# A transformer layer with product-key experts: 672 dense and 352 gathered tokens instead of 704 and 320, five sums kept in PSUM instead of two, gates in DRAM by four blocks

## The chip, the core and the metric

The kernel runs on one core of a Trainium2 chip. The metric is device time in microseconds (us) of the whole program. The engines are TensorE (PE, its weight loads PEld), VectorE (DVE), ScalarE (ACT), GpSimd (POOL) and SyncE (SP), which issues most of the DMAs.

## The reference

One decoder layer on 1024 tokens of width 1024, all in float32. First a modulation from a conditioning vector, a norm, a mixing of tokens (four heads of a gated recurrence, four groups of a short convolution) and its projection. Then the expert layer, which takes most of the time: each token chooses 8 x 16 of 16384 experts by product keys, and each expert is one row of U and one of V:

```python
q = (xb @ w_query).reshape(T, PEER_HEADS, 2, PEER_HALF)
s = jnp.einsum('thpk,hpnk->thpn', q, sub_keys)          # scores of 2 x 128 keys
top_s, top_i = lax.top_k(s, PEER_TOPK)                  # 16 of each half
cand_s = top_s[:, :, 0, :, None] + top_s[:, :, 1, None, :]
best_s, best_pos = lax.top_k(cand_s.reshape(T, PEER_HEADS, -1), PEER_TOPK)
gate = jax.nn.softmax(best_s, axis=-1)
act = jax.nn.gelu(jnp.einsum('td,thkd->thk', xb, u), approximate=False)
return jnp.einsum('thk,thkd->td', gate * act, v)
```

A residual, a second modulation and a final norm close the layer.

## The kernel before

Every large product runs as three products of float32r halves (high x high, high x low, low x high), so one step over 128 channels is three matmuls.

The tokens are treated in two ways. The **dense** ones (the last TD = 704) meet all 128 blocks of 128 experts: a gate matrix that is zero for experts that a token has not chosen is multiplied onto the activations. The **gathered** ones (the first REST = 320) fetch their chosen rows of U and V from DRAM by indirect DMA, 128 rows of 4 KB at a time, one expert for each of up to 128 tokens. A group of 128 tokens needs 128 fetches of U and 128 of V. The last group has only 64 tokens; they are laid twice over the partitions (`dup`), each copy takes half of their experts, and 64 + 64 fetches do; a small matmul (`fold`) adds the copies.

The dense tokens lie in two column parts, `SPL`: 384 columns and the rest. The work goes like this:

- **Mixing** of both halves of the sequence, norms, and the queries of gathered tokens (`query`, on `hg2`).
- **Dense queries and top-k** (lines 873 and 922 to 926).
- **Gates**: 64 tokens at a time (`TG`), one-hot products on TensorE give each token's gates over all 16384 experts; `stg` collects them and one DMA puts them into DRAM (`gd`), in the order in which the main loop reads them back, `GB` blocks of experts at a time. Meanwhile `u_early` computes the activations of 40 blocks (every third) ahead, which wait in DRAM (`ged`).
- **The main loop** over 128 blocks of experts. `u_steps` (line 1161) computes a block's activations for all dense tokens: 24 matmuls into a PSUM bank `pa` for each column part, then Gelu on ScalarE; early blocks come from `ged` instead. `w_step` multiplies by the gates (line 1376, from the buffer `gsb`) and splits the result into `Wh` and `Wl` (lines 113, 114). `v_load` fetches and splits the block's rows of V. After every three blocks (`SB`) comes a **V phase**, `v_phase`: 16 groups (2 column parts x 8 blocks of output channels), each of 9 matmuls (line 1395) into a PSUM bank; VectorE then adds the bank to a sum `acc` in SBUF (line 1411). The sums listed in `FIXED` stay in PSUM banks of their own (`pacc`) for the whole loop and need no addition.
- **The background**, strewn over the main loop by `advance` and `along`: for each gathered row GpSimd issues the fetch into one of five buffers (line 1082, four `grow_` and `more`), and VectorE takes a dot product with the token (line 1100, a u row) or adds the weighted row to a sum (line 1092, a v row).

A scheduler in the recording layer orders the instructions of each engine ahead of time; engines then run their queues in order.

PSUM has eight banks. In the main loop they are two for `pa`, one for each fixed sum, and the others rotate as `pv`:

```python
FIXED = [(0, 0), (1, 0)]
PV = 6 - len(FIXED)
def new_pv():
    return psM.tile([P, 512], F32, name="pv", bufs=PV)
```

Of the kernel before, what the change touches and what calls it, by code (L numbers as in the profile page):

```python
# [7 lines left out]
F32 = mybir.dt.float32  # L8
# [11 lines left out]
P = 128  # L20
# [12 lines left out]
TD = 704  # L33
# [4 lines left out]
GG = [(t, min(P, REST - t)) for t in range(0, REST, P)]  # L38
NG = len(GG)
# the gathered tokens of the last, half tile get their experts together with the half tile of the others  # L40
FULL = REST // P
LAST = REST % P
assert LAST and LAST == P - TD % P
SB = 3
GB = 2
# [9 lines left out]
NF = 2.1  # L55
# [7 lines left out]
FIXED = [(0, 0), (1, 0)]  # L63
# [34 lines left out]
def build(tc, A, out, dbg=None):  # L98
# [12 lines left out]
    def split(hi, lo, src):  # L111
        """two parts of 12 bits each"""
        C.activation(hi, src, AF.Copy)  # L113
        V.tensor_tensor(lo, src, hi.bitcast(F32), op=OP.subtract)  # L114

    def raw_tile(pl, shape, name, lb):
        """float32 values that wait for their split, in a buffer of the low parts"""
        return pl.tile(shape, F32R, name=name + "l", bufs=lb).bitcast(F32)
# [7 lines left out]
    def rsqrt(r, v, tmp, e=0):  # L126
        """of v / 4 ** e: a first guess from the exponent, then Newton steps"""
# [12 lines left out]
    with root:  # L140
# [23 lines left out]
        # ---------------------------------------------------------------- the background  # L164
        # top-k of the gathered tokens, then their experts row by row: steps of it are strewn over the other work;
        # a step yields what it costs VectorE
# [10 lines left out]
        # ---------------------------------------------------------------- stationary operands  # L177
        # all of [P, KC, P], in the order in which TensorE takes them; each is fetched two and split one ahead
# [24 lines left out]
        def halve(n):  # L203
            """there is a third set of halves at times"""
# [7 lines left out]
        def deepen(pl, first, n, every):  # L212
            """that many more from the first on: one of so many goes into a pool of its own"""
# [18 lines left out]
        def ahead():  # L232
            """in the midst of the products with one: split the next"""
# [5 lines left out]
        # ---------------------------------------------------------------- constants, modulation  # L239
# [4 lines left out]
        # three buffers of four row tiles, in turn of the normalised input or w_out, and of the mix or the residual  # L244
# [36 lines left out]
        # TensorE gets to its full clock while the first loads are under way  # L281
# [29 lines left out]
        def mod_part(sec, wa, d):  # L311
            """some columns of a section of the modulation"""
# [5 lines left out]
        def mod_part_rows(sec, wa, d):  # L318
            """the same on TensorE, as a row that is turned into columns"""
# [28 lines left out]
        # ---------------------------------------------------------------- norm 1 and the values  # L348
# [14 lines left out]
        def lnT1(xs, pl, k, h1, onact=False):  # L363
            """transpose a column block of the four row tiles, scale, shift and split it"""
# [16 lines left out]
        def wi_load(pl, k, lb=3, hb=2, ahead=0, wait=[]):  # L381
            """loads run ahead of the splits"""
# [34 lines left out]
        # ---------------------------------------------------------------- projections, token mixing  # L417
# [6 lines left out]
        # lower bounds  # L424
# [16 lines left out]
        # a window of 32 columns of it holds ones in one of them  # L441
# [12 lines left out]
        def mixing(half, mods, h1, og):  # L454
            """projections, recurrence, convolution and group norms of half a sequence, into og"""
# [43 lines left out]
            # blocks of w_in: per head f, q, g (0..11), per conv group c, x, b (12..23)  # L499
# [54 lines left out]
            # masks of the levels: the highest bit in which s and t differ, for s < t  # L554
# [117 lines left out]
            def finish(g):  # L672
                """the scales of a group, from the rows of all of them"""
# [18 lines left out]
        # ---------------------------------------------------------------- w_out, norm 2  # L692
# [4 lines left out]
        def w_out(yp, wop, half, og, finish, between=None, after=None):  # L697
            """the residual after the token mixing, normalised row tiles"""
# [834 lines left out]
```

## Time and profile before

| | us |
|---|---|
| median of 3 runs | 2983.33 (2979.0 to 2987.94) |
| profiled execution, span | 2982.4 (no other time of it is given) |
| TensorE, busy | 2902.0 |
| VectorE, busy | 2524.2 |
| ScalarE, busy | 946.0 |
| GpSimd, busy | 796.2 |
| DRAM read and written | 706.5 MB |

A matmul counts as busy from its start to its modelled end, and neighbours overlap; how fast they follow each other is read from their starts. A VectorE instruction, too, is listed longer than the distance at which the next can start. Busy shares are means over stages with different limits, so the sections below go by stage.

### The profile page before, as it was taken

The page shows a single profiled execution, that of the slowest core. Times are in us where ns is not written, and L with a number is a line of the kernel's source. Part 1 is how long each engine was busy: PE and PEld are TensorE (multiplying, and loading weights), DVE is VectorE, ACT ScalarE, POOL GpSimd, SP SyncE. Part 2 cuts the span into 40 slices and gives each one's busy share as a digit, 9 for nine tenths or more (in the row PEclk, how much of TensorE's full clock was granted, in tenths as well). Part 3 has the DMA queues.
Part 4 walks back from the last instruction along what each step waited for, and adds up shares of the span by engine and source line. Part 5 has one row for each costly group of instructions (what it writes and reads, how often), then busy time and mean ns, then how long its engine had stood idle before and what let it go on. Part 6 is the DMA issues. An engine that isn't in the chain of part 4 may idle for free.

```text
span 2982.4 us, 47131 instructions
## 1 busy us (share of the span) xinstructions
PE 2902.0 (97%) x18242; PEld 2750.8 (92%) x18242; DVE 2524.2 (85%) x5314; ACT 946.0 (32%) x1541; POOL 796.2 (27%) x661
## 2 busy tenths in 40 slices
PE   8999999999999999999999999999999999999998
PEld 6887888878999899999999999999999999999997
DVE  6885559988999877568889989889989988989987
ACT  5643655433122444422222222222222221222221
POOL 0000000000000000015454445435545444444450
PEclk8999999989999999999999999999999999999999
DMA  7424342244223577778889888889889888889883
GB/s 269 146 88 142 130 142 71 85 146 147 61 89 108 181 238 241 234 257 299 302 305 335 314 309 327 320 304 336 304 306 325 319 317 318 307 318 332 304 311 128
DMA packets 286898, 709.65 MB, mean 238 GB/s; under 512 B 26513, under 2 KB 124817, under 8 KB 284370
## 3 DMA queue, kind: packets, MB, share of 16 engines
q1 hardware_dynamic: 192994, 365.56, 35.5%
q0 software_dynamic: 93680, 341.09, 32.2%
q8 instruction: 142, 2.33, 0.3%
q14 instruction: 82, 0.67, 0.1%
HBM read 633.65 MB, written 72.88 MB: 237 GB/s over the span
## 4 chain that ended last, share of the span: by engine, by line
PE 64%; DVE 17%; DMA 10%; issue 5%; ACT 2%; POOL 1%; SPq 0%; DVEq 0%; ACTq 0%; POOLq 0%
PE pv L1395 22%; PE pa L1161 19%; PE pp L467 6%; DMA wl<-in_uT 5%; PE pq L873 4%; PE pacc L1395 3%; DVE wl L114 2%; DMA Wl<-ged 2%; PE ps L577 1%; PE pp L873 1%; PE pg L1327 1%; PE pp L378 1%; DVE gacc L1092 1%; PE pp L714 1%; DVE acc L1411 1%
## 5 line engine op out<-in xcount | busy, mean ns | idle before, releaser
L1161 PE MATMUL pa<-h2h,wh 128*128 128x384 f32 (+1 forms) x1840 | 598.4, 325 | 2.7 <-ACT ge L1166 2.6
L1161 PE MATMUL pa<-h2h,wl 128*128 128x384 f32 (+1 forms) x1840 | 593.9, 323 | 0.0
L1161 PE MATMUL pa<-h2l,wh 128*128 128x384 f32 (+1 forms) x1840 | 593.7, 323 | 0.0
L1395 PE MATMUL pv<-Wh,vh 128*128 128x384 f32 (+1 forms) x1792 | 580.6, 324 | 11.7 <-DVE acc L1411 11.1
L1395 PE MATMUL pv<-Wl,vh 128*128 128x384 f32 (+1 forms) x1792 | 577.3, 322 | 0.0
L1395 PE MATMUL pv<-Wh,vl 128*128 128x384 f32 (+1 forms) x1792 | 577.0, 322 | 0.0
L1395 PEld LDWEIGHTS pv<-Wh,vh 128*128 128x128 f32 x1792 | 336.9, 188 | 22.4 <-DVE acc L1411 19.6
L1161 PEld LDWEIGHTS pa<-h2h,wh 128*128 128x128 f32 x1840 | 346.0, 188 | 4.5 <-ACT ge L1166 3.8
L1161 PEld LDWEIGHTS pa<-h2l,wh 128*128 128x128 f32 x1840 | 346.2, 188 | 0.0
L1161 PEld LDWEIGHTS pa<-h2h,wl 128*128 128x128 f32 x1840 | 346.0, 188 | 0.3 <-DVE wl L114 0.3
L113 ACT ACTIVATE Wh<-Wl 128x704 fp32r<-128x704 f32 x128 | 101.6, 793 | 747.8 <-PE pv L1395 588.2
L1395 PEld LDWEIGHTS pv<-Wh,vl 128*128 128x128 f32 x1792 | 337.0, 188 | 0.0
L1395 PEld LDWEIGHTS pv<-Wl,vh 128*128 128x128 f32 x1792 | 336.9, 188 | 0.0
L113 ACT ACTIVATE wh<-wl 128x1024 fp32r<-128x1024 f32 x187 | 198.0, 1059 | 420.8 <-DMA wl<-in_uT 205.2
L114 DVE TENSOR_TENSOR wl<-wl,wh 128x1024 fp32r<-128x1024 f32 x187 | 227.8, 1218 | 97.7 <-ACT wh L113 95.9
L1411 DVE TENSOR_TENSOR acc<-acc,pv 128x320 f32<-128x320 f32 (+1 forms) x574 | 286.1, 513 | 11.6 <-PE pv L1395 11.3
L114 DVE TENSOR_TENSOR vl<-vl,vh 128x1024 fp32r<-128x1024 f32 x128 | 156.0, 1219 | 18.3 <-ACT vh L113 18.2
L113 ACT ACTIVATE vh<-vl 128x1024 fp32r<-128x1024 f32 x128 | 134.6, 1052 | 79.5 <-DMA vl<-in_v 45.4
L467 PE MATMUL pp<-h1h,wh 128*128 128x512 f32 x384 | 156.6, 408 | 0.0
L467 PE MATMUL pp<-h1h,wl 128*128 128x512 f32 x384 | 152.5, 397 | 3.5 <-DVE wl L114 3.4
L1376 DVE TENSOR_TENSOR Wl<-Wl,gsb 128x704 f32<-128x704 f32 x128 | 113.2, 885 | 48.4 <-DMA Wl<-ged 36.9
L467 PE MATMUL pp<-h1l,wh 128*128 128x512 f32 x384 | 152.3, 397 | 0.0
(1778 smaller groups left out, 5978.2 us busy)
## 6 DMA issues: line engine op xcount, KB each, us to landing
wl<-in_uT SPq DMA_DIRECT2D x128, 512.0 KB
vl<-in_v SPq DMA_DIRECT2D x128, 512.0 KB
gd<-stg SPq DMA_DIRECT2D x11, 4096.0 KB
gsb<-gd SPq DMA_DIRECT2D x64, 704.0 KB
wl<-in_win SPq DMA_DIRECT2D x48, 512.0 KB
wa<-in_wada SPq DMA_DIRECT2D x16, 1024.0 KB
wl<-in_wq SPq DMA_DIRECT2D x32, 512.0 KB
ged<-ge SPq DMA_DIRECT2D x40, 352.0 KB
```

The source lines that it names most:

```text
L113: C.activation(hi, src, AF.Copy)
L114: V.tensor_tensor(lo, src, hi.bitcast(F32), op=OP.subtract)
L378: T.matmul(pvs[t], l[:, t * P:(t + 1) * P], r, start=(k == 0 and l is h1[0][k] and r is wi[0]), stop=(k == KC - 1 and l is h1[1][k]))
L467: T.matmul(pp, l[:, k], r[k], start=(i == 0), stop=(i == 3 * KC - 1))
L577: T.matmul(ps_[:, c], X[:, cs_], Y[:, cs_], start=True, stop=True)
L714: T.matmul(pm, l[:, t * P:(t + 1) * P], r, start=(k == 0 and l is yh[k] and r is woh[k]), stop=(k == KC - 1 and l is yl[k]))
L873: T.matmul(pq[:, :m], l[:, k], hs[k, r][:, o:o + m], start=(i == 0), stop=(i == 3 * KC - 1))
L1092: V.scalar_tensor_tensor(ac, r, aw[:, j:j + 1], ac, op0=OP.mult, op1=OP.add))
L1161: T.matmul(pa[:, :n], l[:, k], h2[k, r][:, o:o + n], start=(i == 0), stop=(i == 3 * KC - 1))
L1376: V.tensor_tensor(gv, gv, gs[b // GB][:, :, b % GB], op=OP.mult)
L1395: T.matmul(pv[:, :n], l[:, c * P:(c + 1) * P], r[:, o:o + n], start=(i == 0 and (not fx or b0 == 0)), stop=(i == 3 * (b1 - b0) - 1 and (no ...
L1411: V.tensor_tensor(a, a, pv[:, :n], op=OP.add)
```

## The change

TD goes from 704 to 672, so the dense parts are 384 and 288 columns, and 352 tokens are gathered. Of these, 96 don't fill a group of 128; they are split into 64 (twice over the partitions) and 32 (four times). There are 352 instead of 320 steps of the background, each one fetch of U and one of V, and a fourth group's end. Gates are built 32 tokens at a time, since 672 is no multiple of 64 tokens; `GB = 4` keeps the runs that they write into DRAM at the same length, and the main loop reads them for four blocks at once. Five sums instead of two stay in PSUM; of the three banks left, one is called `pv` and the two `pa` of `u_steps` serve the V phases too, in turn pa, pa, pv.

```diff
-TD = 704
+TD = 672
-GG = [(t, min(P, REST - t)) for t in range(0, REST, P)]
+GG = [(t * P, P) for t in range(FULL)] + [(t, w) for t, w in ((FULL * P, LAST - LAST % 64), (REST - LAST % 64, LAST % 64)) if w]
-GB = 2
+GB = 4
-NF = 2.1
+NF = 2.1 * TG / 64
-FIXED = [(0, 0), (1, 0)]
+FIXED = [(0, 1), (0, 4), (0, 7), (1, 2), (1, 5)]
...
-        SY.dma_start(idx[lo_, sl], ih[:, :n])
-        SY.dma_start(gkg[lo_, sl], gkf[:, :n])
-        V.tensor_copy(idx[hi_, sl], ih[:, n:])
-        V.tensor_copy(gkg[hi_, sl], gkf[:, n:])
+        for g in range(FULL, NG):
+            o, w = GG[g]
+            r = slice(P - REST + o, P - REST + o + w)
+            n = steps[g]
+            sl = slice(sum(steps[:g]), sum(steps[:g + 1]))
+            for c in range(dup(w)):
+                SY.dma_start(idx[c * w:(c + 1) * w, sl], ih[r, c * n:(c + 1) * n])
+                SY.dma_start(gkg[c * w:(c + 1) * w, sl], gkf[r, c * n:(c + 1) * n])
...
-        PV = 6 - len(FIXED)
+        turn = [0]
         def new_pv():
-            return psM.tile([P, 512], F32, name="pv", bufs=PV)
+            turn[0] = (turn[0] + 1) % 3
+            if turn[0]:
+                return psU.tile([P, 512], F32, name="pa", bufs=2)
+            return psM.tile([P, 512], F32, name="pv", bufs=1)
```

The order on TensorE at the end of a V phase in the middle of the main loop, before; a row is a matmul with the tile that it writes, its operands, the size of its output and, in brackets, the engine that it waits for:

```order
L1395 MATMUL pv<-Wh,vh 128x320 [waits DVE_49]
L1395 MATMUL pv<-Wh,vl 128x320
L1395 MATMUL pv<-Wl,vh 128x320
L1395 MATMUL pv<-Wh,vh 128x320
L1395 MATMUL pv<-Wh,vl 128x320
L1395 MATMUL pv<-Wl,vh 128x320
L1395 MATMUL pv<-Wh,vh 128x320
L1395 MATMUL pv<-Wh,vl 128x320
L1395 MATMUL pv<-Wl,vh 128x320
L1161 MATMUL pa<-h2h_72,wh 128x384 [waits Activation_49]
L1161 MATMUL pa<-h2l_73,wh 128x384
L1161 MATMUL pa<-h2h_72,wl 128x384
```

The same place in the change, in a phase whose last two groups both go into `pa`:

```order
L1403 MATMUL pa<-Wh,vh 128x288
L1403 MATMUL pa<-Wh,vl 128x288
L1403 MATMUL pa<-Wl,vh 128x288
L1403 MATMUL pa<-Wh,vh 128x288
L1403 MATMUL pa<-Wh,vl 128x288
L1403 MATMUL pa<-Wl,vh 128x288
L1403 MATMUL pv<-Wh,vh 128x384 [waits DVE_49,Activation_49]
L1403 MATMUL pv<-Wh,vl 128x384
L1403 MATMUL pv<-Wl,vh 128x384
L1163 MATMUL pa<-h2h_72,wh 128x384 [waits DVE_49]
L1163 MATMUL pa<-h2l_73,wh 128x384
L1163 MATMUL pa<-h2h_72,wl 128x384
```

The first product of U waits for VectorE (an addition out of `pa`) where it waited for ScalarE (an earlier Gelu), and three matmuls of the next V phase, into the free bank `pv`, stand ahead of it.

VectorE's order in the second half of a V phase, before (line 1411 adds a bank to its sum, 1100 is a u row, 1092 a v row; the number behind `grow__` grows with the order in which rows are fetched):

```order
L1100 SCALAR_TENSOR_TENSOR grow__18070,aw<-grow__18070,hx 128x1024 [waits DMASW7_49]
L1411 TENSOR_TENSOR acc_13094<-acc_13094,pv 128x320 [waits PE_49]
L1092 SCALAR_TENSOR_TENSOR gacc<-more,aw,gacc 128x1024 [waits DMASW0_49,DVE_49]
L1411 TENSOR_TENSOR acc_13095<-acc_13095,pv 128x320 [waits PE_49]
L1100 SCALAR_TENSOR_TENSOR grow__18172,aw<-grow__18172,hx 128x1024 [waits DMASW3_49]
L1411 TENSOR_TENSOR acc_13096<-acc_13096,pv 128x320 [waits PE_49]
L1100 SCALAR_TENSOR_TENSOR grow__18109,aw<-grow__18109,hx 128x1024 [waits DMASW1_49]
L1411 TENSOR_TENSOR acc_13097<-acc_13097,pv 128x320 [waits PE_49]
L1411 TENSOR_TENSOR acc_13098<-acc_13098,pv 128x320 [waits PE_49]
```

And in the change, the end of a phase (line 1419 adds, 1102 is a u row, 1094 a v row, 1384 and 116 are W operations):

```order
L1419 TENSOR_TENSOR acc_13120<-acc_13120,pv 128x288 [waits PE_49]
L1384 TENSOR_TENSOR Wl<-Wl,gsb 128x672 [waits DMAHW6_49,DMAHW4_49]
L1419 TENSOR_TENSOR acc_13121<-acc_13121,pa 128x288 [waits PE_49]
L1102 SCALAR_TENSOR_TENSOR grow__18042,aw<-grow__18042,hx 128x1024 [waits DMASW6_49]
L1419 TENSOR_TENSOR acc_13122<-acc_13122,pa 128x288 [waits PE_49]
L1094 SCALAR_TENSOR_TENSOR gacc<-grow__18065,aw,gacc 128x1024 [waits DMASW7_49,DVE_49]
L1419 TENSOR_TENSOR acc_13123<-acc_13123,pv 128x288 [waits PE_49]
L1102 SCALAR_TENSOR_TENSOR grow__18088,aw<-grow__18088,hx 128x1024 [waits DMASW0_49]
L1102 SCALAR_TENSOR_TENSOR more,aw<-more,hx 128x1024 [waits DMASW2_49]
L1419 TENSOR_TENSOR acc_13124<-acc_13124,pa 128x288 [waits PE_49]
L116 TENSOR_TENSOR Wl<-Wl,Wh 128x672 [waits Activation_49]
L1419 TENSOR_TENSOR acc_13125<-acc_13125,pa 128x288 [waits PE_49]
```

Six narrow additions remain in a phase where there were seven, and more row steps stand between them. In the first piece row 18172 (its wait is on DMASW3) is used two places ahead of its turn, before row 18109 (DMASW1); in the second the row in `more` (DMASW2) is one place ahead, since no wait on DMASW1 stands before it.

## Rows read from the trace of the kernel before

**Rows 1.** The head of the page, busy time of TensorE, and the span in 40 slices: the DMA engines' busy tenths and GB/s.

```profile
span 2982.4 us, 47131 instructions
PE 2902.0 (97%) x18242; PEld 2750.8 (92%) x18242; DVE 2524.2 (85%) x5314; ACT 946.0 (32%) x1541; POOL 796.2 (27%) x661
...
DMA  7424342244223577778889888889889888889883
GB/s 269 146 88 142 130 142 71 85 146 147 61 89 108 181 238 241 234 257 299 302 305 335 314 309 327 320 304 336 304 306 325 319 317 318 307 318 332 304 311 128
```

**Rows 2.** Busy time of each engine by stage: from and to, length, then for each engine busy us and (x instructions), granted clock, DMA share, GB/s. In order: queries of gathered tokens, dense queries, top-k with early blocks, gates, the main loop's steady stretch.

```profile
349.00:417.00 68.00, 65.75 (x457) 64.10 (x456) 22.02 (x22) 30.93 (x74) 1.59 (x3) 1.00 0.51 166
690.00:838.00 148.00, 148.00 (x970) 146.76 (x969) 138.60 (x749) 31.62 (x55) 0.00 (x0) 1.00 0.27 90
838.00:985.00 147.00, 138.22 (x827) 134.99 (x827) 143.04 (x625) 38.09 (x60) 0.76 (x1) 0.97 0.31 105
985.00:1255.00 270.00, 260.10 (x2462) 243.03 (x2460) 207.53 (x352) 134.03 (x249) 0.00 (x0) 1.00 0.75 229
1300.00:2900.00 1600.00, 1587.42 (x9841) 1576.90 (x9840) 1434.60 (x2012) 370.99 (x509) 773.21 (x628) 1.00 0.87 314
```

**Rows 3.** Single matmuls in order of time: start, length, line, tiles, size. First and last of 63 with 320 columns; first and last of nine with 384 columns; eight with 128 columns in one row, whose length runs to the end of the last; and that line's lengths (ns, least, median, most).

```profile
1699.72 0.31 PE L1395 MATMUL pv<-Wh,vh 128*128 128x320 f32 x1
...
1708.81 0.31 PE L1395 MATMUL pv<-Wl,vh 128*128 128x320 f32 x1
...
1710.55 0.33 PE L1161 MATMUL pa<-h2h,wh 128*128 128x384 f32 x1
...
1711.94 0.33 PE L1161 MATMUL pa<-h2h,wl 128*128 128x384 f32 x1
...
184.74 1.06 PE L577 MATMUL ps<-X 128*128 128x128 f32 x8
...
L577 PE MATMUL ps<-X x224: 270/275/377, 439.7 to 590.2; 128*128 128x128 f32 x112
```

**Rows 4.** Two lines by themselves, as in rows 2: TensorE's products with V (line 1395) in the main loop, and the gate products (line 1327); busy us and (x instructions) of PE and PEld.

```profile
1262.00:2983.00 1721.00, 1003.87 (x6144) 986.25 (x6144) 1.00 0.85 304
...
985.00:1255.00 270.00, 101.52 (x1408) 81.48 (x1408) 1.00 0.75 229
```

**Rows 5.** VectorE: the additions of line 1411 in the steady stretch (busy us, count); then single instructions in order of time (start, length), for the distance of each to the next.

```profile
1300.00:2900.00 1600.00, 278.96 (x560) 1.00 0.87 314
...
1974.38 0.55 DVE L1411 TENSOR_TENSOR acc<-acc,pv 128x384 f32<-128x384 f32 x1
1974.84 1.22 DVE L1100 SCALAR_TENSOR_TENSOR grow__19937<-grow__19937,hx 128x1024 f32<-128x1024 f32 x1
...
1993.45 0.88 DVE L1376 TENSOR_TENSOR Wl<-Wl,gsb 128x704 f32<-128x704 f32 x1
1994.25 1.22 DVE L114 TENSOR_TENSOR wl<-wl,wh 128x1024 fp32r<-128x1024 f32 x1
...
2218.47 1.28 DVE L1092 SCALAR_TENSOR_TENSOR gacc<-grow__22244,aw,gacc 128x1024 f32<-128x1024 f32 x1
2219.67 0.88 DVE L1411 TENSOR_TENSOR acc<-acc,pv 128x320 f32<-128x320 f32 x2
```

**Rows 6.** The end of a V phase: single instructions of TensorE, then of VectorE, then of GpSimd (start, length; in brackets the idle time before and what ended it).

```profile
1980.98 0.31 PE L1395 MATMUL pv<-Wl,vh 128*128 128x320 f32 x1
1981.13 0.34 PE L1161 MATMUL pa<-h2h,wh 128*128 128x384 f32 x1
...
1977.93 0.48 DVE L1411 TENSOR_TENSOR acc<-acc,pv 128x320 f32<-128x320 f32 x1
1981.90 1.22 DVE L1100 SCALAR_TENSOR_TENSOR grow__20067<-grow__20067,hx 128x1024 f32<-128x1024 f32 x1 [3.50 <-DMA grow__20067<-in_u,idx]
...
1983.06 0.48 DVE L1411 TENSOR_TENSOR acc<-acc,pv 128x320 f32<-128x320 f32 x1
1983.45 1.22 DVE L1100 SCALAR_TENSOR_TENSOR grow__19987<-grow__19987,hx 128x1024 f32<-128x1024 f32 x1
...
1984.60 0.48 DVE L1411 TENSOR_TENSOR acc<-acc,pv 128x320 f32<-128x320 f32 x1
...
1986.14 0.48 DVE L1411 TENSOR_TENSOR acc<-acc,pv 128x320 f32<-128x320 f32 x1
...
1987.69 0.48 DVE L1411 TENSOR_TENSOR acc<-acc,pv 128x320 f32<-128x320 f32 x1
...
1976.34 0.94 POOL L1082 DMA_INDIRECT grow__20067<-in_u,idx  x1 [0.67 <-DVE grow__19937 L1100]
```

**Rows 7.** Who waited for whom in the steady stretch, 1300 to 2900 us: us in total, times, longest. Of VectorE's nine waits for single u rows in `grow_` buffers the longest and the shortest listed; then TensorE's.

```profile
DVE Wl L1376 <- DMA Wl<-ged: 36.9, 15, 6.0
DVE wl L114 <- ACT wh L113: 29.5, 22, 4.1
...
DVE grow__22324 L1100 <- DMA grow__22324<-in_u,idx: 3.6, 1, 3.6
...
DVE grow__15546 L1100 <- DMA grow__15546<-in_u,idx: 2.0, 1, 2.0
...
PE pv L1395 <- DVE acc L1411: 11.1, 13, 2.1
...
PEld pv L1395 <- DVE acc L1411: 19.6, 30, 2.4
```

More of the change, by code (lines that the diff above doesn't have):

```diff
@@ L37 @@
 WT = [min(P, TD - t * P) for t in range(DT)]
-GG = [(t, min(P, REST - t)) for t in range(0, REST, P)]
-NG = len(GG)
 FULL = REST // P
@@ L43 @@
 assert LAST and LAST == P - TD % P
+GG = [(t * P, P) for t in range(FULL)] + [(t, w) for t, w in ((FULL * P, LAST - LAST % 64), (REST - LAST % 64, LAST % 64)) if w]
+assert all(P % w == 0 for _, w in GG)
+NG = len(GG)
 SB = 3
-GB = 2
+GB = 4
 TG = 64 if TD % 64 == 0 else 32
@@ L784, in norm2 @@
                         T.transpose(pr[:w, g], h[:, t:t + w], ident)
-                    full = REST // P
+                    full = FULL
                     if full:
@@ L1236, in build @@
             early_along(pick(new, [a[:, t] for a in ab], ti[:, t], [i1[:, t], i2[:, t]]))
-        lo_, hi_ = slice(0, LAST), slice(P - LAST, P)
-        n = steps[FULL]
-        sl = slice(sum(steps[:FULL]), sum(steps))
-        i1f, i2f, gkf = (a[hi_, DT - 1].rearrange("p k h -> p (k h)") for a in (i1, i2, gk))
-        ih = qp.tile([P, P], I32, name="ih")[hi_]
-        V.scalar_tensor_tensor(ih, i1f, float(NK), i2f, op0=OP.mult, op1=OP.add)
-        SY.dma_start(idx[lo_, sl], ih[:, :n])
-        SY.dma_start(gkg[lo_, sl], gkf[:, :n])
-        V.tensor_copy(idx[hi_, sl], ih[:, n:])
-        V.tensor_copy(gkg[hi_, sl], gkf[:, n:])
+        i1f, i2f, gkf = (a[:, DT - 1].rearrange("p k h -> p (k h)") for a in (i1, i2, gk))
+        ih = qp.tile([P, P], I32, name="ih")
+        V.scalar_tensor_tensor(ih, i1f, float(NK), i2f, op0=OP.mult, op1=OP.add)
+        for g in range(FULL, NG):
[6 more added lines that the diff above has]
+                SY.dma_start(gkg[c * w:(c + 1) * w, sl], gkf[r, c * n:(c + 1) * n])
         stE.close()
```

## The prediction, made before the change was run

> **What bounds the kernel now.** I read the page's first two parts, then busy times by stage, then single matmuls, then VectorE's queue. TensorE is busy for 97% of a span of 2982.4 us [rows 1]. The span has three unlike parts. Before 985 us (mixing, queries, top-k) the engines take turns. From 985 to 1255 us gates are built while early expert blocks fill TensorE. From 1262 us on, 1721 us, the main loop runs, and its steady stretch from 1300 to 2900 us decides: TensorE 1587 of 1600 us at a granted clock of 1.00 (the 2.4 GHz level), VectorE 1434.6 (90%), DMA share 0.87 at 314 GB/s, GpSimd 773 [rows 2]. "Busy" does not say how fast matmuls follow each other, so I take starts: 63 matmuls of 320 columns start 9.09 us apart from first to last, 146.6 ns each; nine of 384 columns take 1.39 us, 173.8 ns each [rows 3]. Sixty-four columns more cost 27.2 ns, 32 columns 13.6; I use 13.3, 32 columns at 2.4 GHz. The loop is bound by columns, with VectorE as a close second: all of TensorE's listed waits there are for VectorE's additions, 11.1 + 19.6 = 30.7 us [rows 7].
>
> **TensorE's terms.** Expert products with U and V are 128 blocks x 48 matmuls each, half of them of the second token part, which shrinks from 320 to 288 columns. For V the trace counts all 6144 [rows 4]. So 3072 + 3072 matmuls save 13.3 ns. In the main loop that is V's 3072 and, for the 88 blocks not done early, 2112 of U: 5184 x 13.3 = 69 us. The 40 early blocks give 960 x 13.3 = 12.8 us; some 17 of them run from 838 to 985 us, where VectorE is busy 143 of 147 us and TensorE 138 [rows 2], so I strike half of those, 2.7 us. Nothing shows a 288-column matmul. Its spacing lies between 112 ns (eight 128-column fp32 matmuls, each with its own weights, take 1.06 us, of which the last one's length is 0.275 us [rows 3]) and 146.6; I take 133, since 320 and 384 lie on one line and 133 is well above the closely spaced rows.
>
> The Trainium skill, "TensorE: Matmul & The Clock Gate", section "Back-to-back issue gap", gives pairs of weight load and matmul a sustained 81 ns at 128 columns and 131 ns at 512. By that slope 32 columns are worth 4.2 ns and the 6144 narrower matmuls 26 us instead of 82. The trace disagrees, 146.6 ns at 320 columns already, and decides.
>
> Gates: 32 tokens fewer, two matmuls each, at 101.52 us / 1408 [rows 4] = 4.6 us. Dense queries: 16 x 24 x 13.3 = 5.1 us, in a stretch where VectorE too is busy 139 of 148 [rows 2]; I count half, 2.5. The gathered queries grow from 320 to 352 columns: 5.1 us back, fully, since TensorE fills 66 of 68 us there [rows 2]. Eight more small transposes and copies in norm 2: 1.5 us, from nothing to twice that. Outside the loop: -12.8 + 2.7 - 4.6 - 2.5 + 5.1 + 1.5 = -10.6 us. Blocks of 32 gate tokens double the number of small VectorE operations there, but VectorE has 62 of 270 us free [rows 2]; without that cover some 3 us.
>
> **VectorE's terms in the loop.** Slots are read from start to start: an eviction takes 0.46 us at 384 columns and 0.40 at 320, a W operation 0.80, a u row 1.15, a v row 1.20 [rows 5, 6]. Of 560 evictions [rows 5] 280 are of each width. Keeping five sums in PSUM instead of two drops 2/7 of the wide (80 x 0.46 = 37 us) and 1/7 of the narrow (40 x 0.40 = 16 us). The other narrow ones lose 32 columns, 0.033 us x 240 = 8; two W operations of 128 blocks lose the same, 8. Together -69 us. Against it stand 32 more row steps, each one u and one v row: 32 x 2.35 = 75 us, and a fourth group's end, about 6. VectorE comes to some 1447 us, 12 more than before, in a stretch that TensorE alone would run in 1600 - 65 = 1535 us (69 x 1600/1698). That is 94% instead of 90%: free time falls from 165 to 88 us, and 36.9 us of it were waits for activations of early blocks on their way back from DRAM and 29.5 for weights [rows 7].
>
> **Where a wait is added.** Before, sums rotate through four banks (pv) and U's products through two others (pa). After, V's sums take pa, pa, pv in turn, three banks in all. Inside a V phase the fixed groups space them out, so a bank is needed again after four or five groups as before; I cost that at nothing, and at 0.5 us for each of 41 phases if not. At the end of a phase it is new: U's first matmul, which found a bank free, now queues behind VectorE's addition for the last but one pa group, and everything on TensorE stands behind it. The trace shows such a handover: U starts 0.15 us after V's last matmul, while VectorE starts the last of the phase's additions at 1987.69, 6.6 us after U, having waited 3.5 us for a gathered row [rows 6]. With eleven turns in a phase and a rhythm of three, in one phase of three the last two sums both lie in pa; there U needs an addition whose products ended only 1.2 us before (nine matmuls of 0.133). In the other two it ended 3.6 us before. Price: from nothing (VectorE in time) to about 5 us (the shown case, in which the last but one addition starts 5.2 us after the last V matmul). I take 1.5 us, nearer the low end since that case stands behind one of only nine u-row waits of 2.0 to 3.6 us [rows 7], for 14 of 41 phases: +21 us.
>
> **The rows.** Five row buffers circulate: VectorE frees one, GpSimd issues the next gather, it lands. The shown row was issued at 1976.34 and used at 1981.90, 5.6 us [rows 6]. Before, 628 rows in 1600 us [rows 2] are 2.55 us a row and 12.7 us for a turn of five; after, 692 in 1535 are 2.22 and 11.1. The lead shrinks by 1.6 us but stays positive; and VectorE's order in the change uses a row two or more places ahead of its turn 8 times (counted over the whole order), before 22 times; the shown wait is of that kind. Half as much again of the 30.7 us that TensorE waits for VectorE: +16 us, between nothing and 60. DMA: 64 more rows of 512 KB are 33.5 MB, gates and early blocks save about 2.4. So 1600 us x 314 GB/s = 502 MB become 533; in 1535 us that is 347 GB/s, share 0.96. The best slice of the page has 336 [rows 1]. With my waits the stretch takes 1572 us and needs 339. I charge no more for DMA; if 336 were a ceiling, the stretch would take 1586 us, 14 more.
>
> **Sum.** 2982.4 - 69 - 10.6 + 21 + 16 = 2939.8, so 2940 us. The page gives the profiled execution no time beside its span; the median of three, 2983.33, lies 0.9 above it, so I leave it. About 0.3% (9 us) is what can be told from no change.
>
> **Rivals.** (a) The waits don't come: VectorE keeps 6% free, U finds its bank, rows land in time: 2982.4 - 79.6 = 2903 us. For it: only 30.7 us of waits at 90%; against: a second engine at 94%. Chance 0.22. (b) The forecast, between 2915 and 2974: 0.52. (c) The gain goes into VectorE and the rows: the loop's rate stays what it was, because the listed DMA waits recur and VectorE has no free time to make them up: 2982.4 - 10.6 = 2972 to 2990. For it: 0.96 DMA share; against: a late VectorE finds its data landed. Chance 0.13. (d) Slower: the bank wait at the handover from V to U. It decides from 79.6 / 41 = 1.9 us in every phase on. At 3 us it gives 2982.4 - 79.6 + 123 = 3026 us. For it: late additions like that in [rows 6]; against: two phases of three leave 3.6 us. Chance 0.11. The Trainium skill, "Perfetto Trace Analysis", section "Matmul Optimizations", asks that all eight banks be leveraged, which speaks for (d): five banks stop rotating here. (e) The matmuls don't shrink with their columns but stay at 146.6 ns: only gates and queries are left, and with the same added waits the time is 2982.4 + 37 = 3019 us. Against it stand two widths on one line [rows 3]. Chance 0.02.
>
> Faster 0.75 ((a), (b), a little of (c)), same 0.12, slower 0.13. For 8 in 10 the range runs from (a) less a little, 2898, up through (c), 2990; that of the likeliest case is 2915 to 2974.
>
> **What would show it.** Spacing of 288-column matmuls near 133 ns; 11 additions in a phase instead of 14; VectorE near 92% and DMA near 340 GB/s in the loop; waits of U's first matmul for the additions, 10 to 40 us in all; no rise of TensorE's waits inside V phases. Wrong would be: U's waits over 60 us, TensorE waiting for W or weights, or VectorE's waits for rows well beyond their present sum.

## The result: slower, 3016 us against 2979

| | before | after |
|---|---|---|
| median of five runs, taken in turn on one chip | 2979.0 us | 3015.95 us (3013.0 to 3030.79) |
| ratio, 95% interval | | 1.0133 [1.0113, 1.0152] |
| profiled execution, its own time | | 3030.79 us (the slowest of the five), span 3029.0 |

The change costs 37 us; 2940 was forecast, 39 us less than before. The profiled execution of after lies 15 us above its median, so its rows tell where time goes, and the sizes below come from medians.

### The profile after

Head of the page and the DMA slices, to be set beside [rows 1].

```profile
span 3029.0 us, 47154 instructions
PE 2864.4 (95%) x18190; PEld 2696.5 (89%) x18190; DVE 2528.4 (83%) x5325; ACT 941.1 (31%) x1549; POOL 890.8 (29%) x726
...
DMA  8324342243123877788989899889898998889894
```

The steady stretch, as the last row of [rows 2].

```profile
1300.00:2900.00 1600.00, 1503.81 (x9438) 1479.01 (x9437) 1383.62 (x1922) 353.57 (x495) 828.01 (x660) 0.98 0.89 319
```

TensorE issues 403 matmuls fewer than before in the same 1600 us (9438 against 9841) and is idle for 96 us instead of 13. VectorE, feared as the next bound, is busy less: 1383.6 us, 86% instead of 90%. So nothing replaced TensorE as the busiest engine; engines wait for each other.

The whole loop: all products with V into sums kept in PSUM (count, least, median and most ns, first and last start).

```profile
L1403 PE MATMUL pacc<-Wh,vh x640: 288/336/446, 1264.4 to 3000.2; 128*128 128x384 f32 x95, 128*128 128x288 f32 x65
```

The same row of before, for the start and the end:

```profile
L1395 PE MATMUL pacc<-Wh,vh x256: 306/334/443, 1282.6 to 2952.7; 128*128 128x384 f32 x85, 128*128 128x320 f32 x43
```

The loop starts 18 us earlier and ends 48 us later in these two executions. All that is lost is lost in the loop.

Who waited for whom in the steady stretch (us in total, times, longest), as [rows 7].

```profile
PEld pa L1163 <- DVE acc L1419: 44.3, 21, 6.9
PE pa L1163 <- DVE acc L1419: 37.9, 18, 6.7
...
PE pa L1403 <- ACT Wl L1168: 25.5, 19, 3.0
...
PE pa L1403 <- DVE acc L1419: 13.7, 17, 2.2
...
PE pv L1403 <- DVE acc L1419: 13.2, 9, 3.4
```

Line 1163 is U's product, 1403 V's, 1168 the Gelu that reads U's result out of its `pa` bank. A PEld row is the same wait seen by the weight load. All four PE rows are waits for a PSUM bank or the engine that empties it: 90 us, against 11.1 us in [rows 7]. The second, at U's start, is the handover of the prediction; the third is its mirror image, V's first sums wanting a `pa` bank that still holds U's result. That one the prediction did not name.

VectorE, for its part, waits longer for gathered rows: over all its lines of such waits in the steady stretch 130 us in 79 waits, against 55 us in 28 before. The lines for the fifth buffer, `more`, two of after and then the longest of before:

```profile
DVE more L1102 <- DMA more<-in_u,idx: 16.4, 7, 6.9
DVE gacc L1094 <- DMA more<-in_v,idx: 14.0, 12, 4.1
...
DVE more L1100 <- DMA more<-in_u,idx: 7.1, 4, 2.9
```

One handover in single instructions (start, length; in brackets the idle time before and what ended it): TensorE, VectorE, GpSimd.

```profile
2149.72 0.29 PE L1403 MATMUL pa<-Wl,vh 128*128 128x288 f32 x1
...
2150.91 0.29 PE L1403 MATMUL pa<-Wl,vh 128*128 128x288 f32 x1
2157.87 0.69 PE L1163 MATMUL pa<-h2h,wh 128*128 128x384 f32 x1 [6.67 <-DVE acc L1419]
2158.35 0.52 PE L1163 MATMUL pa<-h2l,wh 128*128 128x384 f32 x1
2158.67 0.52 PE L1163 MATMUL pa<-h2h,wl 128*128 128x384 f32 x1
```

```profile
2148.05 1.28 DVE L1094 SCALAR_TENSOR_TENSOR gacc<-grow__21447,aw,gacc 128x1024 f32<-128x1024 f32 x1
2156.21 1.23 DVE L1102 SCALAR_TENSOR_TENSOR more<-more,hx 128x1024 f32<-128x1024 f32 x1 [6.89 <-DMA more<-in_u,idx]
...
2157.36 0.45 DVE L1419 TENSOR_TENSOR acc<-acc,pa 128x288 f32<-128x288 f32 x1
2157.73 1.25 DVE L1102 SCALAR_TENSOR_TENSOR grow__21470<-grow__21470,hx 128x1024 f32<-128x1024 f32 x1
```

```profile
2141.95 1.55 POOL L1084 DMA_INDIRECT grow__21470<-in_u,idx  x1 [0.31 <-issue]
...
2145.33 0.94 POOL L1084 DMA_INDIRECT more<-in_u,idx  x1 [0.59 <-DVE gacc L1094]
```

Read it backwards. U's first matmul waits 6.67 us for the addition that frees its `pa` bank. That addition is 0.45 us long, but stands on VectorE behind a row in `more`, which came 10.9 us after its issue (2145.33 to 2156.21). And VectorE's order takes this row ahead of `grow__21470`, issued 3.4 us earlier and used after it. Here a wait of VectorE for DMA becomes a wait of TensorE: U has two `pa` banks, and V's last two sums hold both.

The clock around it (last numbers: granted clock, DMA share, GB/s):

```profile
2145.00:2150.00 5.00, 5.00 (x40) 5.00 (x40) 3.61 (x7) 0.00 (x0) 2.28 (x3) 1.00 0.88 316
2150.00:2157.00 7.00, 1.20 (x10) 0.96 (x8) 0.79 (x1) 1.71 (x2) 0.53 (x1) 0.74 1.01 405
2157.00:2165.00 8.00, 7.13 (x26) 7.13 (x27) 7.91 (x12) 0.02 (x1) 3.82 (x4) 0.59 0.64 212
```

The granted clock was 1.00 up to 2150 us; after the wait it is 0.59: matmuls of 384 columns start 0.32 us apart (2158.35 to 2158.67) instead of the 0.174 of [rows 3].

### The profile page after: what moved, and what is told of

Read it like the earlier page. It is cut to its first block, busy times and chain, and to the rows that moved or that the text cites. A ratio compares the mean times of both kernels' runs of the same rounds, so it can differ in the third digit from the quotient of the medians.

```text
span 3029.0 us, 47154 instructions
## 1 busy us (share of the span) xinstructions
PE 2864.4 (95%) x18190; PEld 2696.5 (89%) x18190; DVE 2528.4 (83%) x5325; ACT 941.1 (31%) x1549; POOL 890.8 (29%) x726
## 4 chain that ended last, share of the span: by engine, by line
PE 29%; DVE 28%; DMA 22%; issue 12%; POOL 5%; ACT 3%; SPq 0%; DVEq 0%; POOLq 0%; ACTq 0%
PE pa L1163 11%; DMA wl<-in_uT 5%; PE pp L469 5%; DMA Wl<-ged 4%; DVE gacc L1094 4%; DVE wl L116 3%; PE pa L1403 2%; PE pg L1330 2%; PE pp L875 2%; DVE acc L1419 2%; DVE vl L116 2%; DMA more<-in_v,idx 1%; DVE Wl L1384 1%; DVE s L926 1%; PE pacc L1403 1%
## 5 line engine op out<-in xcount | busy, mean ns | idle before, releaser
L1403 PE MATMUL pa<-Wh,vh 128*128 128x288 f32 (+1 forms) x941 | 303.3, 322 | 39.6 <-ACT Wl L1168 25.5
L1403 PE MATMUL pa<-Wh,vl 128*128 128x288 f32 (+1 forms) x941 | 298.4, 317 | 0.0
L1403 PE MATMUL pa<-Wl,vh 128*128 128x288 f32 (+1 forms) x941 | 297.8, 316 | 0.0
L1403 PEld LDWEIGHTS pa<-Wh,vh 128*128 128x128 f32 x941 | 179.0, 190 | 53.2 <-ACT Wl L1168 32.4
L1403 PE MATMUL pacc<-Wh,vh 128*128 128x384 f32 (+1 forms) x640 | 206.0, 323 | 1.3 <-ACT vh L115 1.3
L1403 PE MATMUL pacc<-Wh,vl 128*128 128x384 f32 (+1 forms) x640 | 206.2, 322 | 0.5 <-DVE vl L116 0.5
L1403 PE MATMUL pacc<-Wl,vh 128*128 128x384 f32 (+1 forms) x640 | 205.8, 322 | 0.0
L1403 PEld LDWEIGHTS pa<-Wl,vh 128*128 128x128 f32 x941 | 179.3, 191 | 0.4 <-DVE Wl L116 0.3
L1403 PEld LDWEIGHTS pa<-Wh,vl 128*128 128x128 f32 x941 | 179.3, 191 | 0.0
L1403 PE MATMUL pv<-Wh,vh 128*128 128x288 f32 (+1 forms) x467 | 149.2, 319 | 14.9 <-DVE acc L1419 13.4
```

The costliest lines, as they stand in the source:

```text
L1403: T.matmul(pv[:, :n], l[:, c * P:(c + 1) * P], r[:, o:o + n], start=(i == 0 and (not fx or b0 == 0)), stop=(i == 3 * (b1 - b0) - 1 and (no ...
```

## The experiments

Two theories. **Banks**: too few rotating banks make TensorE feel every hold of VectorE. **Rows**: 32 more row steps, fetched and summed, cost more than the forecast 16 us. Every kernel was timed in three rounds beside the kernel before on the same chip; ratios are to that kernel, and differences are of medians unless the text says ratios, by which they come out up to 8 us apart. One warning for all of them: the scheduler makes a new static order for each kernel, and a kernel with fewer fetches came out slower than the one it was cut from (`e11_compute_only_spread` below, by 22 us, 18 by ratios). So a single difference of that size between such kernels is no proof, and that holds for `e4_fixed_last`, `e10_fetch_only_spread` and `e12_six_rows` too; what counts are differences that several kernels show.

### Banks

`e1_own_banks`: the bank code of before in the kernel after, four banks of V's own.

```diff
-FIXED = [(0, 1), (0, 4), (0, 7), (1, 2), (1, 5)]
+FIXED = [(0, 0), (1, 0)]
...
-            turn[0] = (turn[0] + 1) % 3
-            if turn[0]:
-                return psU.tile([P, 512], F32, name="pa", bufs=2)
-            return psM.tile([P, 512], F32, name="pv", bufs=1)
+            return psM.tile([P, 512], F32, name="pv", bufs=PV)   # PV = 6 - len(FIXED)
```

> The changed kernel (672 dense tokens, 352 gathered, gates by four blocks) with the PSUM banks as before: two fixed sums, four banks of their own for the other sums of V, two for U. Theory banks (three banks shared by U and V make TensorE wait for VectorE's additions, and its clock falls after the longer waits): waits in the main loop go back to some 30 us and the clock stays at its upper level, so 2925 us, between 2905 and 2950. Theory VectorE (32 more row steps are too much for it, wherever the banks lie): it gets back 69 us of additions, so it is the bound and the time is 3015 us or more. Theory DMA (64 more gathers of 512 KB make rows and weights late): nothing changes for DMA, 3000 to 3030 us.

2991.66 us, 1.0040 [1.0023, 1.0057]: 24 us of the loss come back by medians (28 by ratios). Its steady stretch and main wait:

```profile
1300.00:2900.00 1600.00, 1525.44 (x9636) 1497.75 (x9635) 1457.10 (x2079) 362.92 (x505) 829.94 (x674) 0.99 0.90 325
...
PE pv L1399 <- DVE acc L1415: 67.1, 46, 5.1
```

Line 1399 is V's product here, 1415 the addition. TensorE still waits 67 us for additions; what went with the shared banks is U's wait for them and V's wait for the Gelu.

`e2_banks_alone` is the reverse: the five kept sums and the shared turn put into the kernel before, 704 tokens.

> The kernel before (704 dense tokens, 320 gathered) with the banks of the change alone: five fixed sums, the other sums of V in turn in pa, pa, pv. Theory banks: waits at the start of U in every third phase as in the change, some 30 us, as much inside V phases and a fallen clock, so 3040 us, between 3010 and 3080. Theory VectorE: it has 53 us less to do than before, so 2979 us or less, down to 2950. Theory DMA: as before, 2979 us.

3002.57 us, 1.0086 [1.0056, 1.0117]: 26 us slower by ratios (21 by medians). Its steady stretch:

```profile
1300.00:2900.00 1600.00, 1571.22 (x9712) 1562.47 (x9711) 1370.83 (x1870) 365.98 (x501) 747.76 (x621) 0.99 0.87 310
```

VectorE is busy 64 us less than in [rows 2], and TensorE gets through 129 matmuls fewer. Taking additions off VectorE gained nothing; the banks it took cost 21 to 26 us. The two runs agree on the size. VectorE's waits for rows are 49 us here and 52 in `e1_own_banks`, no more than the 55 of before; the 130 of after come only where shared banks and 32 more row steps meet.

`e4_fixed_last`: only the choice of kept sums differs, so that no phase ends on two sums in `pa`.

```diff
-FIXED = [(0, 1), (0, 4), (0, 7), (1, 2), (1, 5)]
+FIXED = [(0, 2), (0, 5), (1, 0), (1, 6), (1, 7)]
```

> The changed kernel with other sums fixed: (0,2), (0,5), (1,0), (1,6), (1,7), so that a V phase ends with two groups that need no addition and the last bank that U can ask for is 2.4 us older. Still three shared banks, and the same number of additions. Theory banks: the waits at U's start fall below 10 us, but five groups in a row that need banks, (1,1) to (1,5), wait more inside V; 2975 us, between 2950 and 3000. Theories VectorE and DMA: 3015 us, nothing changes.

2998.29 us, 1.0056 [1.0033, 1.0079].

```profile
PE pa L1403 <- ACT Wl L1168: 37.3, 23, 4.1
...
PE pa L1403 <- DVE acc L1419: 15.6, 26, 2.8
...
PE pv L1403 <- DVE acc L1419: 12.3, 16, 2.0
...
PE pa L1163 <- DVE acc L1419: 0.6, 1, 0.6
```

The handover wait is gone (37.9 to 0.6 us), so its cause is as forecast. But only 18 us of the time came back (23 by ratios): V's start and V's inside still wait, on the same three banks.

Two more on the side of before: `e9_three_fixed` keeps three sums (three rotating banks of V's own, none shared), `e13_one_fixed` one sum (five).

> The kernel before (704 and 320 tokens) with three sums fixed, (0,2), (0,6) and (1,3), and three banks of their own for the others; U keeps its two. VectorE has 41 additions, 19 us, less. Theory VectorE: 2960 us, down from 2981. Theory banks, in the form that the number of rotating banks counts: 2990 to 3005. If only the sharing with U costs: 2965 to 2985.

> The kernel before (704 and 320 tokens) with one sum fixed, (0,0), and five banks for the others. VectorE has 41 narrow additions, 16 us, more. If the number of rotating banks counts as with three of them (31 us slower than four): 2965 us, between 2955 and 2975. If VectorE's load counts more: 2985 to 3000.

3012.41 us, 1.0104 [1.0084, 1.0124], and 2976.52 us, 0.9991 [0.9977, 1.0005]. Sharing is thus not the point, the number is: with 704 tokens three, four and five rotating banks give 3012, 2981 and 2977 us, of which the last two can't be told apart. In `e9_three_fixed` VectorE has again less to do and the kernel is slower. A bank less is always a kept sum more here, so no run separates the two; but a kept sum only takes work away, so the bank costs at least the difference.

### Rows

`e3_no_last_group` leaves the last 32-token group out (its 32 u and 32 v rows, its end); `e8_own_banks_no_last` does that with the banks of `e1_own_banks`.

```diff
-            for g, (o, w) in enumerate(GG):
+            for g, (o, w) in enumerate(GG[:-1]):      # and the same in the background's total
```

> The changed kernel without the rows of its last group of 32 gathered tokens: their expert sums, final norm and store are left out (32 row steps, 64 gathers of 512 KB less). Theory banks: the waits at U's start stay, 2990 us, between 2975 and 3010. Theory VectorE: 82 us of its work are gone, 2935 us, between 2915 and 2960. Theory DMA: 33.5 MB are gone, also 2935 us; this run tells banks from the two others, not those apart.

> The changed kernel with the banks as before (two fixed, four of their own for V) and without the rows of the last group (left out). If the banks (24 us) and the rows (51 us) are separate terms: 2941 us, between 2932 and 2950; that would also show what the narrower products alone are worth, some 40 us to the kernel before, where I counted 80. If both relieve the same wait: 2955 to 2970.

2965.32 us, 0.9954 [0.9938, 0.9970], and 2934.61 us, 0.9849 [0.9827, 0.9871]. The group costs 51 us in one pair (3016 to 2965) and 57 in the other (2992 to 2935), and banks and rows add up. What is left in `e8_own_banks_no_last`, nearly the narrower products alone, is worth 45 us; 80 were forecast.

```profile
1300.00:2900.00 1600.00, 1569.31 (x10042) 1548.90 (x10040) 1438.93 (x2053) 373.38 (x525) 781.18 (x627) 1.00 0.88 313
...
PE pv L1399 <- DVE acc L1415: 22.9, 26, 3.0
```

At 90% of VectorE and a full clock TensorE is idle for 31 us of 1600, 18 more than in [rows 2]: a TensorE that gets faster waits more for VectorE even with no row added. That is half of the missing 35 us. The other half is in the matmuls: busy time for each falls from 1587.42 us / 9841 = 161.3 ns to 156.3, by 5.0 where 6.7 was forecast (13.3 for every second one), and 1.7 ns x 10042 = 17 us. About half of that is the 384-column matmuls, whose starts lie 175 ns apart in the median in every kernel with 672 dense tokens and 173 in every one with 704; no run shows why.

With the group, TensorE's waits for additions go from 22.9 to 67.1 us (`e1_own_banks`). VectorE's waits for rows don't grow with it (66 us in `e8_own_banks_no_last`, 52 in `e1_own_banks`), so with own banks late rows don't carry the 57 us.

What in the rows costs? First the parts of the last group: `e5_fetch_only` fetches its rows but lets VectorE work on 8 of 1024 columns; `e6_compute_only` works in full on `hx` and fetches nothing.

> The changed kernel, all rows fetched, but VectorE works on 8 of the 1024 columns of each row of the last group (32 u and 31 v rows), so that group's result is left out. VectorE has some 67 us less to do, DMA and GpSimd as much as in the change (3016 us). Without that group's rows altogether the time was 2965 us. Theory VectorE (its work on the rows costs the 51 us): 2970 us, between 2955 and 2985. Theory DMA (the 33.5 MB or the turn of the row buffers cost them): 3010 us, between 3000 and 3020.

> The changed kernel with VectorE's whole work on the last group, but on the tokens' own rows instead of fetched ones (64 gathers, 33.5 MB less, that group's result is left out). Theory VectorE: 3010 us, between 3000 and 3020. Theory DMA: 2970 us, between 2955 and 2985. If both matter by half, this run and the one before lie near 2990.

3021.71 us, 1.0134 [1.0112, 1.0156], and 3023.82 us, 1.0121 [1.0082, 1.0159]: neither differs from after. The experiment was badly made: the last group runs at the end of the loop, and the pace of all other background is unchanged. So the same was spread: every eleventh u and v step of all groups (66 of 704).

```diff
-                    r = row(A["v"], j)
+                    r = hx if j % 11 == 5 else row(A["v"], j)         # e11: not fetched
...
+                            r = grow(n) if last else row(A["u"], jj)  # e11: last is jj % 11 == 5
...
+                    m = 8 if j % 11 == 5 else DM                      # e10: 8 columns on VectorE
```

> The changed kernel with all rows fetched, but of every eleventh u and v row of each group (33 of 352 steps, spread evenly) VectorE works on 8 of 1024 columns; the rest of those rows is left out of the result. The runs with the last group alone relieved it only at the end of the loop, while the pace of all rows stayed that of 352 steps. Theory VectorE (its load at that pace): 2970 us, between 2955 and 2990. Theory landing (DMA load, or the turn of the five buffers): 3005 to 3020.

> The changed kernel with VectorE's whole work, but every eleventh u and v row (33 of 352 steps) is not fetched; VectorE takes the tokens' own rows in its place, so the result is not the layer's. 66 gathers, 34.6 MB less, evenly. Theory landing: 2970 us, between 2955 and 2990. Theory VectorE: 3005 to 3020.

3004.51 us, 1.0082 [1.0064, 1.0100], and 3037.49 us, 1.0194 [1.0174, 1.0214]. VectorE relieved: 11 us less. Fetches relieved: 22 us more, which no theory had; why is open. The edit relieves less than its name says: a u step that fetches nothing still writes its product into a `grow_` buffer, so that buffer is not free for the next fetch any earlier. `e20_neither_spread` leaves out both halves of the same 66 steps, at the same pace:

```diff
+                    if j % 11 == 5:
+                        return                                         # v; u likewise, aw gets a one-column copy
```

> The changed kernel, but every eleventh row step of a group is neither fetched nor computed: 33 of 352 u steps and 33 of 352 v steps are left out (a one-column copy stands in for the product's result), strewn over the whole loop, while the pace of the background still counts them. It leaves out as many steps as the kernel without its last group (64), which came to 2965. Theory A, the steps cost as a loop of fetch and sum together: about 2965 to 2975 (41 to 51 us less than 3016). Theory B, it is the pace (how much background the planner spreads over each block) and not the steps themselves: 3005 or more, as with the kernel that fetched all and computed less (3004.5). Theory C, the two parts just add up, -11 of the sums and +22 of the fetches: about 3027.

2986.31 us, 1.0027 [1.0014, 1.0039]: 32 us less than after by ratios, between the numbers of A and B and far from C. One row, fetched and summed, costs 0.48 us (32 / 66), 0.97 us for a step's u and v row, and neither half alone shows it. At that price the group's 64 rows are 31 us; the other 20 or so of the 51 are not in the steps; the pace, the group's own end and the order of the kernel are left, and no run tells them apart.

`e12_six_rows` gives the rows of the main loop a sixth buffer:

```diff
+                    turn_ = taken_rows[0] % (ROWS + 1 + len(sixth))
+                    if turn_ == 1 and sixth:
+                        r = sixth[0].tile([P, DM], F32, name="more2", bufs=1)[:n]
...
```

> The changed kernel with a sixth row buffer in the main loop, so that a turn of the buffers takes 13.3 us at 2.22 us a row instead of 11.1, more than the 12.7 of the kernel before. If late rows cost because the turn is short: 2980 us, between 2965 and 2995. Theory VectorE, or DMA at its limit: 3005 to 3020.

3000.10 us, 1.0052 [1.0025, 1.0078]: 16 us less (24 by ratios). It speaks for the lead of the fetches as part of the cost, in a size at which the order could do it too.

**Bursts.** The shown late row was issued 1.8 us after a load of gates by four blocks, 1344 KB at once (SP's queue in after; start, length):

```profile
2143.49 0.33 SPq L1380 DMA_DIRECT2D gsb<-gd  x1
```

If such loads hold rows up, smaller pieces must help: in three with the change, in three with own banks, in two in the kernel before.

```diff
-            SY.dma_start(gs[q], gd[q])
+            n = slice(NTG * i // PIECES, NTG * (i + 1) // PIECES)
+            SY.dma_start(gs[q][:, n], gd[q][:, n])        # piece i ahead of block i of the four
```

> The changed kernel, with each load of gates for four blocks (1344 KB at once) cut into three of 448 KB, issued at the first three of the four blocks before. Theory burst (a row that is fetched beside such a load lands 2 us later than others, VectorE stands before it, the additions behind it are late, U waits, the clock falls): 2990 us, between 2975 and 3000, and fewer falls of the clock in the loop than 14. Theory pace (rows come every 2.2 us whatever stands beside them): 3010 to 3020.

> The changed kernel with the banks as before (two fixed, four of their own for V; 2992 us) and the loads of gates in three pieces. Theory burst: 2965 us, between 2950 and 2978, faster than the kernel before. Theory pace: 2985 to 2995.

> The kernel before with its loads of gates for two blocks (704 KB) cut into two, one at each block. Theory burst: there TensorE waits only some 30 us for VectorE in the loop, so 2972 us, between 2965 and 2980. Theory pace: 2980, no change.

3024.02 us, 1.0146 [1.0129, 1.0163]; 2992.40 us, 1.0042 [1.0022, 1.0062]; 2978.38 us, 0.9999 [0.9987, 1.0012]. No gain in any of the three pairs: 8 us more, 1 more and no change by medians, with intervals that overlap. The theory falls, and with it the thought that gates by four blocks hurt by their size.

### All banks back

`e17_one_fixed_in_three` has one kept sum and five rotating banks of V's own (`FIXED = [(0, 0)]`, otherwise as `e15_own_banks_in_three`); `e21_none_fixed_in_three` none and six (`FIXED = []`).

> The changed kernel with one fixed sum, five banks of their own for V's other sums, and the loads of gates in three pieces. If the number of rotating banks still counts above four: 5 to 15 us below the same with two fixed and four rotating, so some 2955 us. If VectorE's 41 further additions (16 us) count more: as much above it, some 2975 us.

> 672 dense tokens, gates by four blocks fetched in three pieces, no sum kept in PSUM and so six buffers of their own for the V phase (three shared: 3016, four: 2992, five: 2972). If rotating buffers go on paying: 2955 to 2968. If they have stopped paying, as on the side of 704 tokens (fourth to fifth: 2981 to 2976.5, within 5 us): 2968 to 2976. Rival, VectorE becomes the bound: it was busy 1457 of 1600 us with four and 1491 with five, so about 1525 (95%) here, and the time goes back up to 2980 or more.

2971.86 us, 0.9976 [0.9963, 0.9988], and 2976.09 us, 0.9987 [0.9969, 1.0005]. The first is the only version with all of the work that clearly beats the kernel before, by 7 us; the two can't be told apart. With 672 tokens three (shared), four, five and six rotating banks give 3016, 2992, 2972 and 2976 us. Steady stretch, TensorE's and VectorE's main waits of the one with five, then the stretch of the one with six:

```profile
1300.00:2900.00 1600.00, 1538.51 (x9802) 1516.16 (x9801) 1491.31 (x2139) 368.42 (x518) 828.15 (x684) 0.99 0.92 330
...
PE pv L1403 <- DVE acc L1419: 50.1, 38, 3.4
...
DVE Wl L116 <- ACT Wh L115: 73.3, 45, 4.2
```

```profile
1300.00:2900.00 1600.00, 1533.59 (x9750) 1506.62 (x9748) 1501.98 (x2170) 364.42 (x513) 825.33 (x681) 0.99 0.91 328
```

Here VectorE reaches 93 and 94% and TensorE still waits some 50 us for its additions. 2972 us is the time of rival (c), and a nearly full VectorE is what it named; but the DMA waits that (c) built on don't recur. With five banks VectorE waits 22 us for rows, and 73 us for ScalarE's part in splitting W (the last row above). That this is the kernel's limit is likely, not shown.

## Why the prediction was wrong, point by point

- **The matmuls' length: right.** 288 columns follow at 1.19 / 9 = 0.132 us (2149.72 to 2150.91, ten matmuls); 133 ns was taken. Rival (e) is out. That 69 us shorter matmuls make the loop 69 us shorter was the error: with rows and banks as before only 45 of the 80 us came (`e8_own_banks_no_last`). The prediction let the new waits come from the rows and the handover alone; a faster TensorE against an unchanged VectorE makes waits of its own (18 us there), and the matmuls of 384 columns, which nobody changed, came a little slower. **35 us short.**
- **Outside the loop: right in sign.** The loop's first product with V comes 18 us earlier (one execution each); 10.6 were forecast.
- **"The rows", +16 us: the largest miss.** The last group costs 51 to 57 us (`e3_no_last_group`, `e8_own_banks_no_last`), inside the bounds given (nothing to 60), far from the value taken. "Half as much again of the 30.7 us that TensorE waits for VectorE" fails twice. The 30.7 count the same waits twice, as the weight load's (19.6) and as the matmul's (11.1); TensorE's whole idle time in that stretch is 13 us [rows 2]. And the waits don't grow by half: with own banks they go from 11.1 to 22.9 us by the narrower products and to 67.1 by the group. The sign that the prediction named, VectorE's waits for rows well beyond their sum, came as well, 130 us for 55, but only with the shared banks and the group together. **35 to 41 us short.** Which part of a row costs it is open.
- **"Where a wait is added", +21 us: right in size, in part by luck, and incomplete in place.** 21 to 28 us (`e1_own_banks`, `e2_banks_alone`), 31 without the group (`e3_no_last_group` against `e8_own_banks_no_last`). The handover is real and in the rhythm of three: U's first matmul waits for an addition in 11 of the 13 phases of the steady stretch that end on two sums in `pa` (over 2 us near 1416, 1786, 1904, 2028, 2151 and 2273 us), 28.8 us in all or 2.2 a phase where 1.5 were taken, and in none of the other phases. U's second column part adds 9.2 us, one wait of 3.6 near 1337 among them. All this is gone when the kept sums are placed otherwise. But "inside a V phase ... I cost that at nothing" is wrong: V's products wait 25.5 + 13.7 + 13.2 us in the steady stretch, partly for the Gelu that empties `pa`, and `e4_fixed_last`, where such waits make 65 us, stays at 2998. The net price came out near 21 us though the sum had neither these waits nor what the kept sums take off VectorE. Beside four banks, that is; beside five the change gave away 44 us (3016 to 2972).
- **"VectorE at 94%": wrong for this kernel.** It is at 86%, since it is held by late rows (130 us) and by the other engines in turn. The five kept sums saved its time, which was not what was short. The 94% come true only where all banks rotate (`e21_none_fixed_in_three`).
- **DMA charged nothing:** no run contradicts it as a rate (319 GB/s in the stretch, not the 339 forecast, since the stretch takes longer), and pieces of the gate loads change nothing. As latency it is at the root of the shown handover.
- **Not in the sum at all: the half clock** after a wait (last section).

The misses add up: 35 for the products, 35 to 41 for the rows, 3 to 7 for the banks, 73 to 83 us, where 76 lie between 2940 and 3016. That much was to be expected, since `e8_own_banks_no_last`, `e1_own_banks` and the change are three steps of one path from before; that the bank and the group cost 31 and 51 us in the other order (`e3_no_last_group`) shows that they depend little on each other. The result is on rival (d)'s side, but not rival (d): with 37.9 us of waits at the handover alone the sum would be 2982.4 - 79.6 + 37.9 = 2941 us.

## What to carry to other kernels

A PSUM bank that rotates buys the producer one more group of run-ahead (here 1.2 to 1.6 us, nine matmuls) past a consumer that is now and then held by DMA; before a bank is given to a kept sum, weigh the additions saved against the length of those holds, not against the mean load. Shortening the busiest engine's instructions pays in full only if its partners have time to spare in the same stretch: here 45 of 80 us came, and half of the rest is waits. And where two engines are coupled through few buffers, a falling busy share of both is the sign, so read who waits for whom before reading shares.

## What the hardware showed that was not expected

The granted clock falls in or after TensorE's waits. In the loop of before it is 1.00 in the steady stretch [rows 2]; in after 0.98, in `e1_own_banks` and `e17_one_fixed_in_three` 0.99, in `e8_own_banks_no_last` 1.00, in the order of TensorE's idle time (13, 96, 75, 61 and 31 us of 1600). Not every kernel keeps to that order: `e20_neither_spread` has 0.98 at 66 us, `e14_gates_in_three` 0.99 at 93. In the loop of after there are 15 stretches at the lower of the two levels (1.2 GHz), 75 us together, where before has one of 3.4 us. The longest of TensorE's waits shortly before each of the 15 took between 1.5 and 6.7 us; other waits as long (2.95 us near 1390) have no fall behind them. The one shown comes with a wait of 6.67 us, and the clock is 0.59 over the next 8 us. So a wait is paid twice: 6.67 us idle, then matmuls at 0.32 us instead of 0.174. If all of the 2% fell on work, it would cost 0.02 x 1600 = 32 us; part of it falls on the waits themselves. Worked out from starts, the 217 matmuls that begin in those stretches without a wait of their own come 29 us later in sum than at the spacing of the upper level; in `e1_own_banks` it is 17 us, in before 1.5. By this estimate some 12 us of what the banks cost is clock, in these two executions. No run took the clock's share away by itself.

The Trainium skill, "TensorE: Matmul & The Clock Gate", section "What's actually happening", says that the throttled state is the default and that activity releases it. This trace agrees (1.00 before the shown wait, 0.59 after it).

A gathered row of 512 KB took 10.9 us from issue to use (2145.33 to 2156.21) with VectorE standing ready, against 5.6 us in [rows 6]. The load of the DMA engines alone doesn't tell the two apart: their share was 0.96 (369 GB/s) over the first and 0.93 (333 GB/s) over the second.
